# Depthwise convolution accumulated in a PSUM bank block by block, the MLP product kept in PSUM, the conv norm with tokens on partitions, and the mixer's statistics taken early

## The chip, the cores and the metric

The kernel runs on one core of a Trainium2 chip. Five engines each work through their own queue of instructions in order: TensorE (PE, matrix products and transposes), VectorE (DVE), ScalarE (ACT), GpSimd (POOL), and SyncE (SP), which issues the transfers between HBM and the on-chip SBUF. Matrix products land in PSUM, eight banks of 512 float32 columns on 128 partitions. The metric is device time in microseconds of one execution. The kernel before took 2656.0 us, the median of three runs (2652.93 to 2656.13).

## The reference

One layer of a streaming encoder on 2048 prompt frames and on 8 streams of 16 new frames each, 17 tiles of 128 frames in all, width 1024, all in float32. Cut to what matters here:

```python
hn = rmsnorm(x, norm_mix)
q, k, v, a, g = split(hn @ w_in)            # 512, 128, 128, 512, 512 columns
attn = sliding_window_attention(q, k, v)    # 512 wide; chunks of 64 frames, two chunks back, sinks
u = a * sigmoid(g)                          # GLU
c = depthwise_causal(u, conv_w, conv_b)     # 31 taps, 512 channels
c = silu(layernorm(c, ln_g, ln_b))          # over the 512 channels
x = x + concat(rmsnorm(attn, attn_out_g), rmsnorm(c, conv_out_g)) @ w_out
x = x + square(relu(rmsnorm(x, norm_ffn) @ w_up)) @ w_down      # 4096 wide
x = x + (p @ w_ple) * sigmoid(rmsnorm(x, norm_ple) @ w_ple_gate)
y = rmsnorm(x, final_norm)
```

## The kernel before

Every product is made in three passes: each operand is split into a rounded part and its remainder (ACT rounds, POOL or DVE subtracts: `split`, L120 and L121, for weights as for some activations; `transpose_split` for the normalised input), and high by high, high by low and low by high are added up in one PSUM bank. Activations lie with channels on partitions and frames along the free dimension.

The work goes through stages in this order.

- **A** (about 0 to 250 us): six blocks of up to three tiles. Each is normalised, transposed (`tr`), split (`hn`, L258 and L259), written to the scratch tensor `H`, and multiplied by the `a` and `g` columns of `w_in` in four blocks of 128 channels. ACT takes a tanh (`tg`, L303), DVE makes the GLU (`U`, L314). The weights of this and the next stage come through `raw` (SP, L128) and are split as they arrive; those with a gain, by ACT and DVE (L133, L134).
- **B** (250 to 618 us): the q, k, v columns, from `H` read back as `hnb` (L446 issues eight loads to a block), and attention in 32 chunks of 64 frames: scores (`s`), row maximum (L346, DVE), exponentials (L352, ACT), scaling (L381 and L379: on ACT, DVE, and for the chunks from `TAILC` on also on POOL), transposes (`pt`), values (`o`). The result goes to the scratch tensor `M`.
- **C** (590 to 742 us): the output projection by `c_tile` for nine tiles, 48 products to a tile (L538), each with its two statistics of `M` first: ACT squares (`sq`), POOL adds in two steps, PE sums over partitions (`st`, L528), DVE and POOL make the factor (`ors`). After the fourth tile `mlp_front(0)` reads four finished tiles back from `X1`, scales them (L572) and transposes and splits them (`sp`, `hf`) for the first MLP block.
- **MLP** (742 to 2390 us): five blocks (`F_BLOCKS`), each 32 column blocks of `w_up` (`up`) and their part of `w_down` (`d`). ACT makes relu and its square `ht` (L715, L716), DVE multiplies again in full precision (L717: `relu`<-`up`,`relu`) and subtracts for the remainder (L718). L738 adds `d` to the residual. At the end of block 1 `c_late` does the output projection of the other eight tiles (L623), with its own statistics (`sql`, `stl`, `orl`).
- **PLE** (2390 to 2649 us): the gated embedding and the last norm.

The convolution is a generator (`conv_steps`) that other stages advance. A group is four tiles, 512 frames (or the 8 short streams, `US`); a step is one tap for all four channel blocks. Blocks 0 to 2 are on DVE, each with an accumulator `acc` in SBUF (L201 the first tap, L203 the others: `acc` <- `U` times weight plus `acc`). Block 3 (`PCB`) is an ACT product `tap` (L198) and a POOL addition (L199). After 31 taps `conv_post` transposes a tile (`c`, L152), takes mean and variance (L155, L156, `lrs`), normalises on ACT (`z`, L162), transposes back (L165), applies gain and bias (L169 on DVE for the tiles from `TAILZ` on, else L172 on ACT), tanh and a product (L175, L176), and stores to `M`. `A_STEPS` says how many steps follow each channel block in A, `B_STEPS` how many follow an attention chunk; tiles 9 to 12 and 13 to 16 are done in MLP blocks 0 and 1 (`CONV_LATE`). Both `c` tiles of `conv_post` share the one bank of the pool `psc`.

The order on each engine is fixed when the program is built, by a scheduler with its own model of durations and with priorities from the code (`later`, `steps`); the semaphore waits follow from it.

## Time and profile before

| | |
|---|---|
| median of three runs | 2656.0 us (2652.93 to 2656.13) |
| profiled execution, its own time | 2650.91 us |
| its span, first to last instruction | 2649.1 us |
| mean granted TensorE clock | 0.975 of full speed |
| PE busy | 2527.7 us, 95% |
| DVE, ACT, POOL busy | 1391.0, 1081.8, 1178.6 us |

A busy share says how full an engine was over the whole span and not what the end waited for. The chain that ended last does: it follows each instruction back to what released it. The granted clock is TensorE's share of its full speed; where it is below 1, the same products take longer. In a table by windows, the number of PE instructions in a stretch, held against a stretch in which PE never paused, says how much time was lost there.

### The profile page before, as it was taken

The numbers are of one execution on the slowest core, as the hardware profiler recorded it, in microseconds if no ns is written. First come the engines' busy times: TensorE is split into PE (matmuls) and PEld (weight loads), VectorE is DVE, ScalarE is ACT, GpSimd is POOL, SyncE is SP. The second block draws the span as 40 slices with busy tenths as digits, with TensorE's granted clock in tenths as the row PEclk, the third lists the DMA queues.
The fourth block names the chain that finished last, engine by engine and source line by source line (L and its number), as shares of the span: only waits on it lengthen the run. The fifth ranks groups of instructions, "written<-read, shape, count | busy, mean of one in ns | idle before, by whom it ended". The sixth has DMA issues, their size and how long they took to land.

```text
span 2649.1 us, 32895 instructions
## 1 busy us (share of the span) xinstructions
PE 2527.7 (95%) x12609; PEld 2137.6 (81%) x12609; DVE 1391.0 (53%) x1873; ACT 1081.8 (41%) x2037; POOL 1178.6 (44%) x798
## 2 busy tenths in 40 slices
...
GB/s 233 163 87 150 71 95 60 97 52 116 127 183 79 104 89 114 174 103 92 111 80 129 138 176 169 80 112 80 112 173 128 128 127 199 190 192 126 74 84 48
DMA packets 121854, 320.86 MB, mean 121 GB/s; under 512 B 15713, under 2 KB 49249, under 8 KB 121697
## 3 DMA queue, kind: packets, MB, share of 16 engines
...
HBM read 264.43 MB, written 54.29 MB: 120 GB/s over the span
## 4 chain that ended last, share of the span: by engine, by line
PE 82%; DVE 8%; DMA 3%; POOL 2%; ACT 2%; issue 2%; SPq 0%; POOLq 0%; DVEq 0%; ACTq 0%
PE d L732 26%; PE up L268 24%; PE mm L268 10%; PE pg L754 7%; DVE acc L203 5%; PE acc L538 4%; PE accl L623 2%; PE o L398 2%; PE pq L761 2%; PE s L370 1%; POOL acc L199 1%; POOL w L121 1%; DVE ht L718 1%; ACT pr L352 1%; PE pt L392 1%
## 5 line engine op out<-in xcount | busy, mean ns | idle before, releaser
L121 POOL TENSOR_TENSOR w<-raw,w 128x1024 fp32r<-128x1024 f32 x305 | 767.0, 2531 | 656.9 <-ACT w L120 617.4
L732 PE MATMUL d<-w,ht 128*128 128x512 f32 x3264 | 768.6, 393 | 23.6 <-DVE ht L718 20.3
L268 PE MATMUL up<-hf,w 128*128 128x512 f32 (+2 forms) x3840 | 762.5, 357 | 1.1 <-POOL w L121 1.0
L732 PEld LDWEIGHTS d<-w,ht 128*128 128x128 f32 x3264 | 613.0, 189 | 153.7 <-DVE ht L718 23.0
L268 PEld LDWEIGHTS up<-hf,w 128*128 128x128 f32 x3840 | 659.2, 189 | 93.6 <-POOL w L121 1.4
L120 ACT CAST w<-raw 128x1024 fp32r<-128x1024 f32 x330 | 345.6, 1049 | 637.5 <-PE d L732 445.8
L203 DVE SCALAR_TENSOR_TENSOR acc<-U,vec,acc 128x512 f32<-128x512 f32 x360 | 416.9, 1206 | 0.0
L738 DVE TENSOR_TENSOR accf<-d,accf 128x512 f32<-128x512 f32 x272 | 175.2, 685 | 322.7 <-PE d L732 322.2
L718 DVE TENSOR_TENSOR ht<-relu,ht 128x512 fp32r<-128x512 f32 (+2 forms) x160 | 246.1, 1538 | 5.3
L717 DVE SCALAR_TENSOR_TENSOR relu<-up,relu 128x512 f32<-128x512 f32 (+2 forms) x160 | 97.0, 606 | 236.8 <-ACT ht L716 236.5
L199 POOL TENSOR_TENSOR acc<-acc,tap 128x512 f32<-128x512 f32 (+1 forms) x150 | 198.2, 1321 | 38.5 <-ACT tap L198 29.0
L268 PE MATMUL mm<-hn,w 128*128 128x384 f32 (+1 forms) x1152 | 204.5, 335 | 5.8 <-ACT tg L303 3.7
L268 PE MATMUL mm<-hnb,w 128*128 128x256 f32 (+1 forms) x1152 | 180.4, 306 | 21.0 <-DMA hnb<-H 17.6
L268 PEld LDWEIGHTS mm<-hn,w 128*128 128x128 f32 x1152 | 194.3, 193 | 7.0 <-ACT tg L303 4.2
L268 PEld LDWEIGHTS mm<-hnb,w 128*128 128x128 f32 x1152 | 157.7, 195 | 35.3 <-issue 27.2
L715 ACT ACTIVATE relu<-up 128x512 f32<-128x512 f32 (+2 forms) x160 | 84.9, 531 | 196.2 <-PE up L268 193.4
L754 PE MATMUL pg<-w,xg 128*128 128x512 f32 x510 | 125.4, 392 | 0.0
L198 ACT ACTIVATE tap<-U,vec 128x512 f32<-128x512 f32 x120 | 86.1, 725 | 77.5 <-POOL acc L199 77.0
L754 PEld LDWEIGHTS pg<-w,xg 128*128 128x128 f32 x510 | 94.6, 188 | 18.8
L623 PE MATMUL accl<-w,msl 128*128 128x512 f32 x384 | 94.7, 404 | 9.4 <-DVE xcl L628 9.2
L538 PE MATMUL acc<-w,ms 128*128 128x512 f32 x384 | 94.1, 404 | 7.1 <-ACT ms L120 7.1
L623 PEld LDWEIGHTS accl<-w,msl 128*128 128x128 f32 x384 | 73.8, 195 | 25.3 <-DVE xcl L628 9.4
...
## 6 DMA issues: line engine op xcount, KB each, us to landing
raw<-in_w_up SPq DMA_DIRECT2D x160, 512.0 KB, 3.5
raw<-in_w_down SPq DMA_DIRECT2D x160, 512.0 KB, 3.5
...
```

The lines of the kernel that those rows point to most:

```text
L120: nc.scalar.copy(hi, src)
L121: (eng or nc.gpsimd).tensor_tensor(lo, src, hi.bitcast(F32), ALU.subtract)
L199: nc.gpsimd.tensor_tensor(acc, acc, t, ALU.add)
L203: nc.vector.scalar_tensor_tensor(acc, v, w_, acc, ALU.mult, ALU.add)
L268: nc.tensor.matmul(ps, w(wp, k), m[:, ap_, 0:n], start=(i == 0), stop=(i == 3 * KD - 1))
L538: nc.tensor.matmul(ps, ms[:, ap_, k, :], wo[k][:, wp, nh * 512:(nh + 1) * 512], start=(i == 0), stop=(i == 11))
L623: nc.tensor.matmul(pd[nh], ms[h][:, ap_, k, :], wo[4 * h + k][:, wp, nh * 512:(nh + 1) * 512], start=(i == 0), stop=(i == 11))
L717: nc.vector.scalar_tensor_tensor(r[:, 0:n], ps[:, 0:n], 0.0, r[:, 0:n], ALU.max, ALU.mult)
L718: hs = nc.vector.tensor_tensor(ht[:, 1, 0:n], r[:, 0:n], ht[:, 0, 0:n].bitcast(F32), ALU.subtract)
L732: nc.tensor.matmul(pd[nh], hts[f][:, hp, i * P:(i + 1) * P], wds[f][:, wp, nh * 512:(nh + 1) * 512], start=(j == 0), stop=(j == 3 * GRP - 1))
L738: ad = nc.vector.tensor_tensor(xs, pd[nh], xs, ALU.add)
L754: nc.tensor.matmul(pg, xg[ap_][:, k * P:(k + 1) * P], wg[k][:, wp, ns], start=(i == 0), stop=(i == 3 * KD - 1))
```

## The change

- `conv_steps`: the three DVE blocks are no longer advanced together. Their 93 taps are taken in the order block 0, taps 0 to 30, then block 1, then block 2, still three to a step. The running sum is in the bank `c` of `psc` (a new tile for each block), and only the last tap of a block writes `acc` in SBUF. Each tap now reads what the tap just before it wrote. Block 3 stays on ACT and POOL as it was.
- `conv_post`: gain and bias lie as rows (`lnr`, a new 512 KB input that is spread over the partitions and halved on POOL at the start), so the norm, tanh and product are done with tokens on partitions, by three DVE instructions in or out of the bank (L159, L161, L163), with tanh and a square with sum on ACT between. The sum of squares gives the second statistic of the mixer (`ors[:, t, 1]`). Then come one set of transposes back (L169) and one ACT copy.
- `attn_stat`: after each pair of attention chunks, and once for the short streams, ACT squares `mta` into a `pt` bank, DVE sums over four (L450), PE sums over partitions (L452), DVE and POOL make the factor (L453, L454). It is done 17 times.
- `c_tile` and `c_late_front` lose their statistics and read `ors`. `c_tile` takes its inputs from buffers of its own, and `mlp_front(0)` now follows its seventh tile (tile 8 and tile 0 come after it).
- MLP: the product of L717 goes into the `up` bank in place of `relu`, and the subtraction reads it there.
- `A_STEPS` for the last block falls from 2 to 1, and `B_STEPS` becomes two steps after each chunk.

```diff
-A_STEPS = {1: 4, 2: 4, 3: 2, 4: 2, 5: 2}
-B_STEPS = (1, 2)
+A_STEPS = {1: 4, 2: 4, 3: 2, 4: 2, 5: 1}
+B_STEPS = (2, 2)
...
-        nm = cpool.tile([P, 1], F32, name="lnm")
-        nc.vector.scalar_tensor_tensor(nm, mv[:, 0:1], -1.0, rs, ALU.mult, ALU.mult)
+        nc.vector.scalar_tensor_tensor(tp, tp, mv[:, 0:1], lnr[:, 0], ALU.subtract, ALU.mult)
         z = cpool.tile([P, CC], F32, name="z", bufs=1)
-        nc.scalar.activation(z, tp, AF.Identity, bias=nm, scale=rs)
+        nc.vector.scalar_tensor_tensor(z, tp, rs, lnr[:, 1], ALU.mult, ALU.add)
+        nc.scalar.activation(tp, z, AF.Tanh)
+        nc.vector.scalar_tensor_tensor(z, tp, 1.0, z, ALU.add, ALU.mult)
+        ss = cpool.tile([P, 1], F32, name="lss")
+        nc.scalar.activation(tp, z, AF.Square, accum_out=ss)
+        rstd(ors[:, t, 1:2], ss, 1.0 / CC)
         zt = psc.tile([P, CC], F32, name="c")
         for cb in range(4):
             nc.tensor.transpose(zt[:, cb * P:(cb + 1) * P], z[:, cb * P:(cb + 1) * P], ident)
-        zc = cpool.tile([P, 4, P], F32, name="zc", bufs=1)
-        for cb in range(4):
-            if t >= TAILZ:
-                nc.vector.tensor_scalar(zc[:, cb, :], zt[:, cb * P:(cb + 1) * P], g_lg[:, cb:cb + 1],
-                                        g_lb[:, cb:cb + 1], ALU.mult, ALU.add)
-            else:
-                nc.scalar.activation(zc[:, cb, :], zt[:, cb * P:(cb + 1) * P], AF.Identity,
-                                     bias=g_lb[:, cb:cb + 1], scale=g_lg[:, cb:cb + 1])
-        th = cpool.tile([P, 4, P], F32, name="th", tag="z", bufs=1)
-        nc.scalar.activation(th, zc, AF.Tanh)
-        nc.vector.scalar_tensor_tensor(zc, th, 1.0, zc, ALU.add, ALU.mult)
+        zc = cpool.tile([P, 4, P], F32, name="zc", tag="z", bufs=1)
+        nc.scalar.copy(zc.rearrange("p k n -> p (k n)"), zt)
         nc.sync.dma_start(M[t][:, 4:8, :], zc)
...
-        tall = [cpool.tile([P, 512], F32, name="acc", bufs=5) for _ in range(4)]
+        tall = [cpool.tile([P, 512], F32, name="acc", bufs=4) for _ in range(4)]
         accs = [shape(x) for x in tall]
+        def view(cb, j):
+            if tiles[0] == 0:
+                return US[:, cb, :, j:j + DS]
+            return U[c0 // 512][:, cb, c0 % 512 + j:c0 % 512 + j + n]
+
+        own = [(cb, j) for cb in range(4) if cb not in PCB for j in range(KC)]
+        per = len(own) // KC
         for j in range(KC):
-            for cb in range(4):
-                v = US[:, cb, :, j:j + DS] if tiles[0] == 0 else U[c0 // 512][:, cb, c0 % 512 + j:c0 % 512 + j + n]
+            for cb in PCB:
                 w_, acc = cw[:, j, cb:cb + 1], accs[cb]
-                if cb in PCB:
-                    if j == 0:
-                        nc.gpsimd.tensor_scalar(acc, v, w_, g_b[:, cb:cb + 1], ALU.mult, ALU.add)
-                    else:
-                        t = shape(cpool.tile([P, 512], F32, name="tap", align_bytes=ALN))
-                        nc.scalar.activation(t, v, AF.Copy, scale=w_)
-                        nc.gpsimd.tensor_tensor(acc, acc, t, ALU.add)
-                elif j == 0:
-                    nc.vector.tensor_scalar(acc, v, w_, g_b[:, cb:cb + 1], ALU.mult, ALU.add)
+                if j == 0:
+                    nc.gpsimd.tensor_scalar(acc, view(cb, j), w_, g_b[:, cb:cb + 1], ALU.mult, ALU.add)
                 else:
-                    nc.vector.scalar_tensor_tensor(acc, v, w_, acc, ALU.mult, ALU.add)
+                    t = shape(cpool.tile([P, 512], F32, name="tap", align_bytes=ALN))
+                    nc.scalar.activation(t, view(cb, j), AF.Copy, scale=w_)
+                    nc.gpsimd.tensor_tensor(acc, acc, t, ALU.add)
+            for cb, i in own[j * per:(j + 1) * per]:
+                w_ = cw[:, i, cb:cb + 1]
+                if i == 0:
+                    pacc = shape(psc.tile([P, CC], F32, name="c"))
+                    nc.vector.tensor_scalar(pacc, view(cb, i), w_, g_b[:, cb:cb + 1], ALU.mult, ALU.add)
+                else:
+                    nc.vector.scalar_tensor_tensor(accs[cb] if i == KC - 1 else pacc, view(cb, i), w_, pacc,
+                                                   ALU.mult, ALU.add)
             yield
...
+    nc.sync.dma_start(lnr, a["lnr"].partition_broadcast(P))
+    nc.gpsimd.tensor_scalar(lnr, lnr, 0.5, None, ALU.mult)
...
+    def attn_stat(t, mta):
+        sq = psb.tile([P, 512], F32, name="pt").rearrange("p (j n) -> p j n", j=4)
+        nc.scalar.activation(sq, mta, AF.Square)
+        sr = bpool.tile([P, P], F32, name="sra", bufs=1)
+        nc.vector.tensor_reduce(sr, sq.rearrange("p j n -> p n j"), AX.X, ALU.add)
+        st = psb.tile([P, 512], F32, name="pt")
+        nc.tensor.matmul(st[:, 0:1], sr, ones[:, 0:1], start=True, stop=True)
+        nc.vector.tensor_scalar(ors[:, t, 0:1], st[:, 0:1], 1.0 / CC, EPS, ALU.mult, ALU.add)
+        nc.gpsimd.tensor_tensor(ors[:, t, 0:1], ors[:, t, 0:1], mhalf[:, 0:1], ALU.pow)
...
+                attn_stat(1 + (c0 + i) // 2, mta)
     nc.sync.dma_start(M[0][:, 0:4, :], mts)
+    attn_stat(0, mts)
...
-        nc.scalar.activation(sq, mt, AF.Square)
-        s4 = sq.rearrange("p (h k) n -> p h k n", h=2)
-        nc.gpsimd.tensor_tensor(s4[:, :, 0:2], s4[:, :, 0:2], s4[:, :, 2:4], ALU.add)
-        nc.gpsimd.tensor_tensor(s4[:, :, 0], s4[:, :, 0], s4[:, :, 1], ALU.add)
-        st = ps_.tile([P, 512], F32, name="st", **stt)
-        for h in range(2):
-            nc.tensor.matmul(st[:, h:h + 1], s4[:, h, 0], ones[:, 0:1], start=True, stop=True)
-        rs = pl.tile([P, 2], F32, name="ors", bufs=2)
-        nc.vector.tensor_scalar(rs, st[:, 0:2], 1.0 / CC, EPS, ALU.mult, ALU.add)
-        nc.gpsimd.tensor_tensor(rs, rs, mhalf, ALU.pow)
...
-                nc.vector.scalar_tensor_tensor(xs, ps, rs[:, h:h + 1], xs, ALU.mult, ALU.add)
+                nc.vector.scalar_tensor_tensor(xs, ps, ors[:, t, h:h + 1], xs, ALU.mult, ALU.add)
...
-        c_tile(t, opool, ps2, hpool.tile([P, 8, P], F32, name="mt", tag="xnf", bufs=XNB),
-               hpool.tile([P, D], F32, name="xc", tag="xnf", bufs=XNB),
-               opool.tile([P, 2, 8, P], F32R, name="ms", align_bytes=ALN),
-               opool.tile([P, 8, P], F32, name="sq"), dict(bufs=1), dict(bufs=4))
-        if t == F_BLOCKS[0][-1]:
+        c_tile(t, opool, ps2, opool.tile([P, 8, P], F32, name="mt"), opool.tile([P, D], F32, name="xc"),
+               opool.tile([P, 2, 8, P], F32R, name="ms", align_bytes=ALN), dict(bufs=4))
+        if t == F_BLOCKS[1][-2]:
             mlp_front(0, ps2, "sp", 2)
...
-            sq = fpool.tile([P, 4, P], F32, name="sql", tag="relu", bufs=2)
-            nc.scalar.activation(sq, mt[:, 4 * h:4 * h + 4], AF.Square)
-            nc.gpsimd.tensor_tensor(sq[:, 0:2], sq[:, 0:2], sq[:, 2:4], ALU.add)
-            nc.gpsimd.tensor_tensor(sq[:, 0], sq[:, 0], sq[:, 1], ALU.add)
-            nc.tensor.matmul(st[:, h:h + 1], sq[:, 0], ones[:, 0:1], start=True, stop=True)
-        rs = fpool.tile([P, 2], F32, name="orl", bufs=2)
-        nc.vector.tensor_scalar(rs, st[:, 0:2], 1.0 / CC, EPS, ALU.mult, ALU.add)
-        nc.gpsimd.tensor_tensor(rs, rs, mhalf, ALU.pow)
-        return xt, ms, rs
-
-    def c_late_half(h, xt, ms, rs):
+        return xt, ms
...
-                nc.vector.scalar_tensor_tensor(r[:, 0:n], ps[:, 0:n], 0.0, r[:, 0:n], ALU.max, ALU.mult)
-                hs = nc.vector.tensor_tensor(ht[:, 1, 0:n], r[:, 0:n], ht[:, 0, 0:n].bitcast(F32), ALU.subtract)
+                nc.vector.scalar_tensor_tensor(ps[:, 0:n], ps[:, 0:n], 0.0, r[:, 0:n], ALU.max, ALU.mult)
+                hs = nc.vector.tensor_tensor(ht[:, 1, 0:n], ps[:, 0:n], ht[:, 0, 0:n].bitcast(F32), ALU.subtract)
```

What this does to the order is shown at three places. The first is DVE at the end of A, around the last three GLU products (`U_140` before, `U_141` after, buffer `U3` in both). Before:

```order
L314 SCALAR_TENSOR_TENSOR U_140<-tg,mm 128x256
L203 SCALAR_TENSOR_TENSOR acc<-U_137,vec,acc 128x512 x6
L314 SCALAR_TENSOR_TENSOR U_140<-tg,mm 128x256
L203 SCALAR_TENSOR_TENSOR acc<-U_137,vec,acc 128x512 x8
L134 SCALAR_TENSOR_TENSOR w<-raw,vec,w 128x1024
L314 SCALAR_TENSOR_TENSOR U_140<-tg,mm 128x256
```

After, `c` is the bank that holds the running sum:

```order
L320 SCALAR_TENSOR_TENSOR U_141<-tg,mm 128x256
L207 SCALAR_TENSOR_TENSOR c<-U_138,vec,c 128x512 x5
L320 SCALAR_TENSOR_TENSOR U_141<-tg,mm 128x256
L207 SCALAR_TENSOR_TENSOR c<-U_138,vec,c 128x512 x5
L134 SCALAR_TENSOR_TENSOR w<-raw,vec,w 128x1024
L320 SCALAR_TENSOR_TENSOR U_141<-tg,mm 128x256
```

Eighteen taps stood between the first of these GLU products and the last; now there are twelve.

The second place is POOL. Before, the additions of tiles 9 to 12 (`acc`) stand between the weight remainders `w` of MLP block 0:

```order
L195 TENSOR_SCALAR acc<-U_139,vec 128x512
L199 TENSOR_TENSOR acc<-acc,tap 128x512 x2
L121 TENSOR_TENSOR w<-raw,w 128x1024
L199 TENSOR_TENSOR acc<-acc,tap 128x512
L121 TENSOR_TENSOR w<-raw,w 128x1024 x2
L199 TENSOR_TENSOR acc<-acc,tap 128x512
L121 TENSOR_TENSOR w<-raw,w 128x1024
L199 TENSOR_TENSOR acc<-acc,tap 128x512
L121 TENSOR_TENSOR w<-raw,w 128x1024 x2
L199 TENSOR_TENSOR acc<-acc,tap 128x512
```

After, the same additions stand in the last chunks of attention, around the softmax scalings `pr`:

```order
L387 TENSOR_SCALAR pr<-pr,rc 128x192
L200 TENSOR_TENSOR acc<-acc,tap 128x512
L454 TENSOR_TENSOR ors<-ors,mhalf 128x1
L101 TENSOR_SCALAR ors<-lss 128x1
L200 TENSOR_TENSOR acc<-acc,tap 128x512
L102 TENSOR_TENSOR ors<-ors,mhalf 128x1
L387 TENSOR_SCALAR pr<-pr,rc 128x192
L200 TENSOR_TENSOR acc<-acc,tap 128x512 x4
L387 TENSOR_SCALAR pr<-pr,rc 128x192
L200 TENSOR_TENSOR acc<-acc,tap 128x512 x3
L454 TENSOR_TENSOR ors<-ors,mhalf 128x1
L200 TENSOR_TENSOR acc<-acc,tap 128x512 x9
```

and MLP block 0 begins like this:

```order
L121 TENSOR_TENSOR w<-raw,w 128x1024 x3
L101 TENSOR_SCALAR rs_121<-oss 128x1
L121 TENSOR_TENSOR w<-raw,w 128x1024
L102 TENSOR_TENSOR rs_121<-rs_121,mhalf 128x1
L121 TENSOR_TENSOR w<-raw,w 128x1024 x55
```

The thirty additions (and their ACT products) moved from MLP block 0 to the end of B, and five of the six softmax scalings on POOL now have two to twelve of them directly in front. Before, no addition stood between those six.

The third place is PE in C, around the transposes `sp` of `mlp_front(0)`. Before:

```order
L538 MATMUL acc<-w,ms 128x512 x33
L256 MATMUL sp<-ident,xnf 128x128 x32
L538 MATMUL acc<-w,ms 128x512 x34
L528 MATMUL st<-ones,sq 128x1 x2
L538 MATMUL acc<-w,ms 128x512 x14
```

After:

```order
L546 MATMUL acc<-w,ms 128x512 x44
L261 MATMUL sp<-ident,xnf 128x128 x8
L546 MATMUL acc<-w,ms 128x512 x24
L261 MATMUL sp<-ident,xnf 128x128 x4
L546 MATMUL acc<-w,ms 128x512 x4
L261 MATMUL sp<-ident,xnf 128x128 x4
L546 MATMUL acc<-w,ms 128x512 x20
L261 MATMUL sp<-ident,xnf 128x128 x4
L546 MATMUL acc<-w,ms 128x512 x3
L261 MATMUL sp<-ident,xnf 128x128 x4
L546 MATMUL acc<-w,ms 128x512 x45
L273 MATMUL up<-hf,w 128x512 x50
```

The 32 transposes stood in one piece with four tiles of products still to come; now they come in small groups between the products of the last tiles, and the small products `st` are gone.

## Rows read from the trace of the kernel before

**Rows 1.** The page: busy share of PE, and the chain that ended last.

```profile
PE 2527.7 (95%) x12609; PEld 2137.6 (81%) x12609; DVE 1391.0 (53%) x1873; ACT 1081.8 (41%) x2037; POOL 1178.6 (44%) x798
...
PE 82%; DVE 8%; DMA 3%; POOL 2%; ACT 2%; issue 2%; SPq 0%; POOLq 0%; DVEq 0%; ACTq 0%
```

**Rows 2.** By window: bounds, length, busy time of each engine (x instructions), granted clock, DMA.

```profile
140.00:160.00 20.00, 20.00 (x123) 19.93 (x122) 18.50 (x22) 7.78 (x14) 15.21 (x11) 1.00 0.19 70
160.00:180.00 20.00, 13.97 (x61) 13.04 (x60) 19.08 (x18) 11.19 (x21) 15.27 (x10) 0.74 0.12 44
...
229.00:251.00 22.00, 4.07 (x30) 3.69 (x30) 22.00 (x26) 3.81 (x5) 7.69 (x4) 0.68 0.46 149
...
540.00:618.00 78.00, 67.03 (x257) 39.47 (x257) 40.88 (x105) 44.46 (x155) 13.25 (x16) 0.82 0.14 53
618.00:742.00 124.00, 104.55 (x465) 85.14 (x464) 38.43 (x60) 40.79 (x60) 50.64 (x52) 0.89 0.39 132
...
776.00:880.00 104.00, 88.88 (x369) 71.31 (x368) 95.19 (x72) 43.62 (x58) 89.25 (x43) 0.92 0.28 97
880.00:1103.00 223.00, 223.00 (x1010) 184.67 (x1009) 140.12 (x166) 70.33 (x92) 106.12 (x48) 1.00 0.29 101
...
1176.00:1200.00 24.00, 16.80 (x65) 12.82 (x65) 17.15 (x12) 11.92 (x17) 24.00 (x11) 0.86 0.40 144
...
1436.00:1549.00 113.00, 99.05 (x439) 81.48 (x438) 39.54 (x67) 34.24 (x67) 54.69 (x74) 0.94 0.42 145
```

**Rows 3.** DVE by line and form: busy, mean ns of one | idle before, released by.

```profile
L203 DVE SCALAR_TENSOR_TENSOR acc<-U,vec,acc 128x512 f32<-128x512 f32 x360 | 416.9, 1206 | 0.0
...
L738 DVE TENSOR_TENSOR accf<-d,accf 128x512 f32<-128x512 f32 x272 | 175.2, 685 | 322.7 <-PE d L732 322.2
...
L718 DVE TENSOR_TENSOR ht<-relu,ht 128x512 fp32r<-128x512 f32 x96 | 144.8, 1508 | 3.1
...
L542 DVE SCALAR_TENSOR_TENSOR xc<-acc,ors,xc 128x512 f32<-128x512 f32 x32 | 23.4, 748 | 28.6 <-PE acc L538 22.6 <-POOL ors L531 3.3 <-POOL rs L102 2.4
```

**Rows 4.** The taps of L203 alone, in two windows: length, DVE busy (x taps).

```profile
500.00:600.00 100.00, 25.31 (x36) 0.86 0.23 77
...
780.00:870.00 90.00, 61.47 (x34) 0.92 0.27 93
```

**Rows 5.** Timeline at the end of A: start, length, engine, line, what.

```profile
230.13 5.61 POOL L121 TENSOR_TENSOR w<-raw,w 128x1024 fp32r<-128x1024 f32 x2
230.98 7.96 DVE L203 SCALAR_TENSOR_TENSOR acc<-U,vec,acc 128x512 f32<-128x512 f32 x6
...
234.79 0.36 ACT L303 ACTIVATE tg<-mm 128x256 f32<-128x256 f32 x1
...
245.69 0.40 DVE L314 SCALAR_TENSOR_TENSOR U<-tg,mm 128x256 f32<-128x256 f32 x1
...
246.17 4.53 SPq L446 DMA_DIRECT2D hnb<-H  x8
...
250.53 0.98 PE L268 MATMUL mm<-hnb,w 128*128 128x384 f32 x2 [16.29 <-DMA hnb<-H]
```

**Rows 6.** Chain in C, in order of time: start, length, what.

```profile
639.40 11.47 PE acc L538 x50
...
665.90 4.37 DMA xnf<-X
...
684.46 5.67 PE acc L538 x18
```

**Rows 7.** What PE waited for from 1430 to 1552 us: total, times, longest.

```profile
PE accl L623 <- DVE xcl L628: 9.2, 2, 7.0
PE stl L611 <- POOL sql L610: 4.6, 1, 4.6
```

**Rows 8.** Block 3's ACT products and POOL additions by form.

```profile
L199 POOL TENSOR_TENSOR acc<-acc,tap 128x512 f32<-128x512 f32 x120 | 184.2, 1535 | 31.1 <-ACT tap L198 24.0 <-DVE acc L203 0.6 <-ACT va L490 0.3
...
L198 ACT ACTIVATE tap<-U,vec 128x512 f32<-128x512 f32 x120 | 86.1, 725 | 77.5 <-POOL acc L199 77.0
```

26 lines of the change are left out of this document (13 added, 13 removed).

## The prediction

> **What bounds the kernel now.** I read the page's busy shares and its chain first: PE is busy 95% of the span and is 82% of the chain, DVE 8% [rows 1]. So a change that takes no products away can only win back the time in which PE stood or ran at a lowered clock. The table by windows says where that is. A stretch in which PE never paused gives the rate: 1010 instructions in 223 us, 4.53 per us [rows 2]. Held against it (the reader is to see the instruction count, not the busy time, since a lowered clock also stretches busy time):
> - 776 to 880 us (MLP block 0): 369 / 4.53 = 81.5, so 22.5 of 104 us lost; DVE is busy 95.19 of it.
> - 618 to 742 (C): 465 / 4.53 = 102.6, 21.4 lost.
> - 1436 to 1549 (the late output projection): 439 / 4.53 = 96.9, 16.1 lost.
> - 1176 to 1200 (block 1): 65 / 4.53 = 14.3, 9.7 lost.
> - 160 to 180 (A; its shorter products give 123 in the 20 us before): 20 x 61 / 123 = 9.9, 10.1 lost.
> - 229 to 251: PE has little to do; the wait ends at 250.53 with `hnb` [rows 5].
> - 540 to 618 (the end of B): 257 instructions of mixed length at a clock of 0.82; about 11 us idle, more by clock [rows 2].
>
> **The taps.** The by-form view has 360 taps of 512 columns at a mean of 1206 ns, 416.9 us of DVE [rows 3]. That mean hides two prices: 25.31 / 36 = 0.70 us in a window where POOL does little, 61.47 / 34 = 1.81 us in block 0, where POOL is busy 89.25 of 104 us [rows 2, 4]. The subtraction L718, which like a tap takes both its tensors from SBUF, has 1508 ns; L738 and L542, which take one from PSUM, have 685 and 748 ns [rows 3], and L738 runs in that same block. So what is slow is a DVE instruction with two SBUF tensors beside a busy POOL, and after the change a tap has one SBUF tensor and one PSUM tensor.
>
> No row of before shows an instruction of DVE that writes PSUM, nor a tap that reads what the tap just before it wrote. Bounds: 0.685 us (L738) below, 1.81 us (the crowded tap, no relief) above. The nearest row in form is L542 (a pointer scalar, PSUM and SBUF in): 0.748 us; with some hundredths for the wait on the tap before, I take 0.80. 360 x (1.206 - 0.80) = 146 us of DVE go. Nearly all of that lay beside PE's work; it is worth only what PE waited for.
>
> [...]
>
> **The sum, stage by stage, against the profiled execution's 2650.9 us.**
> - 160 to 180: DVE held back GLU and `hn` by runs of taps. At 0.80 in place of the mean of 1.206 a run of six takes 4.8 us for 7.2, and two such runs stand in it; 7 of the 10.1 us come back (bounds 3 and 10).
> - End of A: the eight `hnb` loads stand on SP behind a weight load that waits for DVE, and DVE reaches its last GLU product at 245.69, six taps before it taking 7.96 us from 230.98 on, 1.33 each [rows 5]. Between the first and the last of the three GLU products in the first listing of the change, 18 taps become 12. From 230.98, twelve at 0.80, the GLU products and a weight's remainder (some 2 us) end at about 243 at worst; at best nothing of DVE is late, and POOL's remainders end it at 235.74, just behind the last tanh at 235.15. The 4.53 us of the loads behind that give PE its first product between 240.5 and 247 in place of 250.53: 7 us (3 to 10).
> - B: of the 102 steps of the first three groups (31 taps each and 9 tiles) A does 52 in place of 56, so B gets 50 in place of 46, which hardly counts; what is new is in its last 78 us. Block 3's work for tiles 9 to 12 comes here: 30 ACT products at 0.725 = 22 us beside the 44.46 that ACT has, and 30 POOL additions at 1.535 = 46 us beside 13.25 [rows 2, 8]. Five of the six softmax scalings on POOL stand behind two to twelve additions, and PE's transposes wait for them. In return tiles 5 to 8 are convolved earlier, so DVE is freer. The 17 `attn_stat` add each one ACT square, one DVE sum, a PE instruction of one column; at 0.73 and 0.75 us they fit into what ACT and DVE have idle even at the end of B, 33.5 and 37.1 us of 78 [rows 2], but take `pt` banks. Bounds: +8 us won (the DVE taps are gone) and 25 us lost (twelve additions at 1.535 = 18 us late once, and some products). I take 6 lost.
> - C: the pause from the end of the fourth tile's products to 684.46 comes from storing the tile, reading it back (4.37 us) and the transposes behind it [rows 6]. With two more tiles of products behind `mlp_front(0)` (96 x 11.47 / 50 = 22 us) it is covered, and the adds and `st` products of eight tiles go. Of 21.4 us lost, the wait for the first tile's load at 618 stays: 18 won (10 to 24).
> - Block 0: groups of three taps at 1.81 = 5.4 us stand in front of L717 and L718, which PE waits for; at 0.80 they are 2.4. POOL has no additions left here. 20 of 22.5 us (9 to 22).
> - Block 1: the POOL additions stay, so only the DVE part: 5 of 9.7 (0 to 9.7).
> - Late projection: PE waited 9.2 us for `xcl` and 4.6 for the last `sql` addition [rows 7]. The second goes whole, of the first the part that stood behind the statistics' POOL work. The loads behind the four buffers stay: 10 of 16.1 (4 to 16).
> - L717 and L718: 96 subtractions of 512 columns get a PSUM source, about 0.75 for 1.508 us; PE is full in 880 to 1103 with the old price [rows 2], so nothing beyond the blocks above. What the longer use of an `up` bank costs: L718 now ends earlier than before, so nothing.
> - Conv norm: DVE gets two more instructions of 512 columns for tiles before 9, fewer for the others. Two waits (POOL's root, ACT's tanh) stand in DVE's queue, where before three did for the late tiles. 0.
> - Start: 512 KB more to load while the weights come: 2 lost (0 to 3).
>
> 7 + 7 - 6 + 18 + 20 + 5 + 10 - 2 = 59 us. 2650.9 - 59 = 2591.9; the profiled execution lies 5.1 us below the median of the runs, so on the median's scale 2656 - 59 = 2597 us. All bounds at their good end make 10 + 10 + 8 + 24 + 22 + 9.7 + 16 = 100 us, 2556; all at their bad end 3 + 3 - 25 + 10 + 9 + 0 + 4 - 3 = 1, 2655.
>
> **The rivals.**
> 1. *The tap keeps its price.* One tensor and the weights are still read from SBUF, and if a tap that waits for its forerunner costs 1.2 us, A's and block 0's gains fall to a third, block 1's to nothing. Left: 2 + 3 - 10 + 18 + 7 + 0 + 10 - 2 = 28 us, 2628. For it: no row shows a DVE write to PSUM, and each tap now waits. Against it: L738 and L542.
> 2. *The whole loss comes back.* The end of B gains from the freed DVE instead of losing, and C and the late projection come near their bounds: 2562 to 2570. For it: PE's rows at 880 to 1103 show that nothing else is short. Against it: chains of loads in C and in the late projection that the change leaves.
> 3. *DVE in B becomes the bound: slower.* Taps stand between row maximum, scale and reciprocal of each chunk on an engine that works in order, and 150 of them are a chain now. At 1.5 us for a tap, B's 150 take 150 x 0.80 = 120 us more of DVE than at 0.70; half of it on PE's path is 60 us lost, against 44 won elsewhere (A, block 0 and block 1 at a half, 3 + 3 + 10 + 2, with C's 18, the late projection's 10 and the start's 2 off): 2656 + 16 = 2672. It decides from 44 / 75 + 0.70 = 1.29 us for a tap. For it: the end of B hangs on latency, its clock is 0.82. Against it: DVE is busy only 40.88 of 78 us there [rows 2].
> 4. *The change doesn't do what it says in block 0*, because POOL's weight remainders were the bound there all along: 89.25 of 104 us. Then 10 of the 20 us stay lost: 2607, inside the forecast's range.
>
> **How the numbers follow.** Forecast with rival 4 (2575 to 2615): 0.60. Rival 1 (2615 to 2640): 0.16. Rival 2 (below 2575): 0.13. No change within 0.2% (5 us, about what a measurement can tell): 0.04. Rival 3 and like losses: 0.07. Range 2562 to 2638: it leaves out the best part of rival 2 and all above rival 1. Faster 0.89, same 0.04, slower 0.07.
>
> **What would show it.** Taps of L207 near 0.8 us alike beside a busy and an idle POOL; if they are above 1.2 in block 0, rival 1. PE's counts in MLP block 0 at 4.5 per us throughout. The first `hnb` product between 241 and 247. In C no pause of 20 us, and the stage near 105 us. At the end of B the wait of PE for `pr`: over 10 us more than before means that the term for B is wrong. A stage B (now 367 us) of more than 390 would make the whole forecast wrong.

## The result and the profile after

The changed kernel took 2563.6 us, the median of four runs (2561.82 to 2565.52), against 2656.1 beside it: a ratio of 0.9653, 95% interval 0.9637 to 0.967. The forecast was 2597 us in a range of 2562 to 2638. So the direction was right and the gain larger than forecast, 92.5 us for 59; the time lies at the very edge of the range, below the 2575 to 2615 that the forecast held likeliest.

The page after, its busy shares and its chain:

```profile
PE 2503.8 (98%) x12575; PEld 2120.4 (83%) x12575; DVE 1115.8 (44%) x1874; ACT 1060.9 (41%) x2027; POOL 1084.7 (42%) x783
...
PE 94%; ACT 2%; DMA 2%; DVE 1%; POOL 1%; issue 1%; SPq 0%; POOLq 0%; ACTq 0%; DVEq 0%
```

PE now fills 98% of the span and is 94% of the chain; DVE, 8% of it before [rows 1], is down to 1%. The work by window (length, busy time of each engine (x instructions), granted clock, DMA):

```profile
160.00:180.00 20.00, 20.00 (x126) 19.79 (x125) 16.89 (x27) 16.79 (x29) 17.90 (x18) 1.00 0.46 171
231.00:532.00 301.00, 287.80 (x1786) 230.94 (x1787) 174.41 (x403) 183.70 (x605) 54.91 (x61) 0.97 0.27 87
532.00:620.00 88.00, 69.39 (x268) 41.09 (x267) 40.64 (x99) 64.87 (x183) 52.65 (x60) 0.78 0.17 59
620.00:712.00 92.00, 92.00 (x416) 75.87 (x416) 35.71 (x46) 23.29 (x32) 27.25 (x24) 0.98 0.47 164
780.00:880.00 100.00, 100.00 (x443) 82.81 (x442) 57.04 (x82) 25.17 (x32) 40.05 (x17) 1.00 0.27 90
1374.00:1464.00 90.00, 90.00 (x406) 74.42 (x405) 35.32 (x48) 28.51 (x59) 41.14 (x50) 1.00 0.52 182
```

These answer to [rows 2]: the stretch of A that ran at a clock of 0.74 is full at 1.00, 100 us of MLP block 0 hold 443 instructions, 4.43 per us, C and the late projection have no gap. Only B is worse: at its end, 532 to 620 us, the clock is 0.78 for 0.82, with 64.87 us of ACT and 52.65 us of POOL where there were 44.46 and 13.25, and before that PE is idle for 13 of 301 us.

DVE by line and form:

```profile
L207 DVE SCALAR_TENSOR_TENSOR c<-U,vec,c 128x512 f32<-128x512 f32 x348 | 261.3, 751 | 6.1
L735 DVE TENSOR_TENSOR accf<-d,accf 128x512 f32<-128x512 f32 x272 | 176.1, 686 | 386.7 <-PE d L729 386.1
...
L715 DVE TENSOR_TENSOR ht<-up,ht 128x512 fp32r<-128x512 f32 x96 | 66.3, 691 | 54.2 <-ACT ht L713 51.6
...
L550 DVE SCALAR_TENSOR_TENSOR xc<-acc,ors,xc 128x512 f32<-128x512 f32 x32 | 24.0, 749 | 32.3 <-PE acc L546 31.8
...
L450 DVE TENSOR_REDUCE sra<-pt 128x128 f32<-128x512 f32 x17 | 11.6, 684 | 5.9 <-ACT pt L448 5.9
```

and the taps alone in three windows (DVE busy (x taps)), the second and third in the MLP blocks:

```profile
160.00:240.00 80.00, 43.68 (x58) 0.91 0.47 161
740.00:900.00 160.00, 50.38 (x67) 1.00 0.31 105
1100.00:1400.00 300.00, 62.80 (x84) 1.00 0.31 105
```

The reader is to hold these against [rows 3, 4]: 0.753, 0.752 and 0.748 us for a tap, the same everywhere. The 0.70 and 1.81 us that the prediction reads from [rows 4] are busy time divided by a count. Taps that overlap, or that the edge of the window cuts, make that quotient a little low; by line and form the taps of before in the same two windows have

```profile
L203 DVE SCALAR_TENSOR_TENSOR acc<-U,vec,acc 128x512 f32<-128x512 f32 x36 | 25.4, 746 | 0.0
...
L203 DVE SCALAR_TENSOR_TENSOR acc<-U,vec,acc 128x512 f32<-128x512 f32 x34 | 62.3, 1882 | 0.0
```

So a tap took 746 ns where POOL was busy 10.03 of 100 us and 1882 where it was busy 82.93 of 90, and now takes 751 on average. The subtraction fell from 1508 to 691 ns. What the chain of taps costs is seen from start to start. A run of three in the kernel before and a run of six after, by the timeline:

```profile
544.72 2.05 DVE L203 SCALAR_TENSOR_TENSOR acc<-U,vec,acc 128x512 f32<-128x512 f32 x3
...
204.26 4.71 DVE L207 SCALAR_TENSOR_TENSOR c<-U,vec,c 128x512 f32<-128x512 f32 x6
```

Before, (2.05 - 0.74) / 2 = 0.66 us: each tap started before the last had ended. After, (4.71 - 0.75) / 5 = 0.79 us, so waiting for the tap before costs 0.13 us a link.

The end of A, by the timeline:

```profile
222.50 0.36 ACT L309 ACTIVATE tg<-mm 128x256 f32<-128x256 f32 x1
...
223.83 0.41 DVE L320 SCALAR_TENSOR_TENSOR U<-tg,mm 128x256 f32<-128x256 f32 x1
...
224.32 6.30 SPq L462 DMA_DIRECT2D hnb<-H  x8
...
231.36 0.98 PE L273 MATMUL mm<-hnb,w 128*128 128x384 f32 x2 [9.83 <-DMA hnb<-H]
```

DVE's last GLU product now starts 1.0 us behind the end of its tanh (10.5 us before, [rows 5]); the eight loads follow at once, and 7 us later PE has its first `hnb`, at 231.36 us, earlier than the 241 to 247 that the prediction named as a sign. What PE waits for over the whole run, the two lines that the text uses:

```profile
PE mm L273 <- DMA hnb<-H: 11.9, 4, 9.8
...
PE pt L452 <- DVE sra L450: 8.2, 4, 2.9
```

The gain by stage, from the first and last starts of PE's products (their lines in the trace; us). The two columns of A are up to the last product with `hn`, and from there to the first with `hnb`; B ends with the first product of C on `ms`, C with the first `up`, blocks 0 and 1 with the first product of the late projection.

| run | A | end of A | B | C | blocks 0, 1 | late proj. | rest | span |
|---|---|---|---|---|---|---|---|---|
| before | 234.0 | 16.5 | 373.6 | 118.7 | 693.5 | 112.4 | 1100.4 | 2649.1 |
| after | 221.3 | 10.1 | 388.3 | 92.5 | 662.4 | 88.8 | 1100.3 | 2563.7 |
| e1_taps_sbuf | 230.7 | 12.8 | 406.3 | 92.6 | 662.5 | 88.8 | 1100.2 | 2593.9 |
| e2_before_taps_psum | 222.8 | 9.8 | 360.4 | 120.9 | 663.0 | 115.4 | 1100.2 | 2592.5 |
| e3_product_sbuf | 220.4 | 9.5 | 387.7 | 93.8 | 661.8 | 89.4 | 1100.7 | 2563.3 |
| e4_stats_late | 220.7 | 10.7 | 357.2 | 103.1 | 664.9 | 118.7 | 1100.2 | 2575.5 |
| e5_stat_one_pair_later | 221.5 | 10.5 | 379.1 | 93.4 | 662.2 | 88.8 | 1100.4 | 2555.9 |
| e6_late_adds_held | 220.4 | 10.2 | 383.1 | 93.6 | 662.3 | 88.8 | 1099.2 | 2557.6 |
| e6b_late_adds_held_taps_sbuf | 230.3 | 12.7 | 395.1 | 93.0 | 675.9 | 88.8 | 1100.6 | 2596.4 |
| e6c_held_all_sbuf | 230.8 | 12.7 | 395.9 | 93.5 | 681.4 | 90.6 | 1101.7 | 2606.6 |
| e7_front_after_fourth | 220.7 | 9.5 | 391.5 | 92.3 | 662.2 | 88.8 | 1099.1 | 2564.1 |
| e10_late_stats_in_mlp | 221.7 | 9.3 | 364.0 | 111.7 | 666.8 | 88.8 | 1101.1 | 2563.4 |
| e11_stat_later_adds_held | 221.0 | 10.8 | 370.5 | 93.9 | 662.5 | 88.9 | 1102.8 | 2550.4 |
| e12_front_fourth_shared_xnf | 221.1 | 10.8 | 391.3 | 115.4 | 662.3 | 88.8 | 1099.6 | 2589.3 |

Between the profiled executions 85.4 us went: 12.7 in A, 6.4 at its end, 26.2 in C, 31.1 in the blocks, 23.6 in the late projection, less 14.7 in B. B is the one stage that the change made longer. Among the four kernels of the table whose code for B is the same (after, e3, e7, e12) B varies from 387.7 to 391.5 us, so a few microseconds there say nothing.

The `up` products tell the two blocks apart: from the first of block 0 to the first of block 1, which is the 769th of them, PE took 376.6 us before and 355.8 after, and from there to the late projection 316.9 and 306.6.

### The profile page after: what moved, and what is told of

Same layout as the page of the kernel before. It is cut to its first block, busy times and chain, and to the rows that moved or that the text cites. A ratio compares the mean times of both kernels' runs of the same rounds, so it can differ in the third digit from the quotient of the medians.

```text
span 2563.7 us, 32974 instructions
## 1 busy us (share of the span) xinstructions
PE 2503.8 (98%) x12575; PEld 2120.4 (83%) x12575; DVE 1115.8 (44%) x1874; ACT 1060.9 (41%) x2027; POOL 1084.7 (42%) x783
## 4 chain that ended last, share of the span: by engine, by line
PE 94%; ACT 2%; DMA 2%; DVE 1%; POOL 1%; issue 1%; SPq 0%; POOLq 0%; ACTq 0%; DVEq 0%
PE up L273 29%; PE d L729 29%; PE mm L273 12%; PE pg L751 7%; PE acc L546 4%; PE accl L620 3%; PE o L404 2%; PE pq L758 2%; PE s L376 1%; DMA hnb<-H 1%; PE pt L398 1%; PE tr L661 1%; PE tr L261 1%; PE pt L392 0%; PE up L261 0%
## 5 line engine op out<-in xcount | busy, mean ns | idle before, releaser
L121 POOL TENSOR_TENSOR w<-raw,w 128x1024 fp32r<-128x1024 f32 x305 | 731.5, 2412 | 708.5 <-ACT w L120 707.2
L729 PE MATMUL d<-w,ht 128*128 128x512 f32 x3264 | 759.7, 390 | 0.3 <-ACT ht L713 0.3
L207 DVE SCALAR_TENSOR_TENSOR c<-U,vec,c 128x512 f32<-128x512 f32 x348 | 261.3, 751 | 6.1
L714 DVE SCALAR_TENSOR_TENSOR up<-up,relu 128x512 f32<-128x512 f32 (+2 forms) x160 | 98.9, 618 | 311.9 <-ACT relu L712 311.7
L200 POOL TENSOR_TENSOR acc<-acc,tap 128x512 f32<-128x512 f32 (+1 forms) x150 | 169.3, 1129 | 44.5 <-ACT tap L199 33.9
L715 DVE TENSOR_TENSOR ht<-up,ht 128x512 fp32r<-128x512 f32 (+2 forms) x160 | 97.7, 611 | 109.8 <-ACT ht L713 105.8
L454 POOL TENSOR_TENSOR ors<-ors,mhalf 128x1 f32<-128x1 f32 x17 | 10.5, 616 | 196.3 <-DVE ors L453 196.2
L713 ACT ACTIVATE ht<-relu 128x512 fp32r<-128x512 f32 (+2 forms) x160 | 90.6, 566 | 1.3
```

The lines of the kernel that those rows point to most:

```text
L121: (eng or nc.gpsimd).tensor_tensor(lo, src, hi.bitcast(F32), ALU.subtract)
L200: nc.gpsimd.tensor_tensor(acc, acc, t, ALU.add)
L207: nc.vector.scalar_tensor_tensor(accs[cb] if i == KC - 1 else pacc, view(cb, i), w_, pacc, ALU.mult, ALU.add)
L713: nc.scalar.activation(ht[:, 0, 0:n], r[:, 0:n], AF.Square)
L714: nc.vector.scalar_tensor_tensor(ps[:, 0:n], ps[:, 0:n], 0.0, r[:, 0:n], ALU.max, ALU.mult)
L715: hs = nc.vector.tensor_tensor(ht[:, 1, 0:n], ps[:, 0:n], ht[:, 0, 0:n].bitcast(F32), ALU.subtract)
```

## The experiments

**The sum back in SBUF, alone.** In the changed kernel:

```diff
-                    pacc = shape(psc.tile([P, CC], F32, name="c"))
-                    nc.vector.tensor_scalar(pacc, view(cb, i), w_, g_b[:, cb:cb + 1], ALU.mult, ALU.add)
+                    nc.vector.tensor_scalar(accs[cb], view(cb, i), w_, g_b[:, cb:cb + 1], ALU.mult, ALU.add)
...
-                    nc.vector.scalar_tensor_tensor(accs[cb] if i == KC - 1 else pacc, view(cb, i), w_, pacc,
-                                                   ALU.mult, ALU.add)
+                    nc.vector.scalar_tensor_tensor(accs[cb], view(cb, i), w_, accs[cb], ALU.mult, ALU.add)
```

> The changed kernel with one thing undone: the running sum of a channel block lies in SBUF (acc) again, block by block as after the change. Theory (the price of a tap with two SBUF tensors beside a busy POOL is what held PE in A and in MLP blocks 0 and 1, and the PSUM operand takes it away): taps at 1.2 to 1.8 us where POOL is busy, 0.75 to 0.80 where it is idle, PE short again in A and in block 1 at least; 10 us back in A and 15 to 25 in the blocks, 2590 to 2600 us. Rival (the gain came from the order: block 3's additions moved out of block 0, fewer steps at the end of A): taps slow, but hidden beside PE; 2564 to 2572 us.

It took 2598.0 us, ratio to before 0.9783 (0.9766 to 0.9799). The total is the theory's, its places only in part: of 30.2 us of span, 9.4 + 2.7 are in A, as expected, but the other 18.0 lie in B and none in the blocks. The taps alone, by window (DVE busy (x taps)):

```profile
500.00:600.00 100.00, 20.94 (x29) 0.95 0.27 91
740.00:900.00 160.00, 73.43 (x57) 1.00 0.39 132
1100.00:1400.00 300.00, 123.34 (x90) 1.00 0.32 107
```

Slow again beside POOL, 1.29 and 1.37 us in the blocks (POOL busy 86.53 us of the 155 from 745 on, and 161.92 of 300), and yet PE stayed full there: it was busy for all of both stretches, with 685 and 1331 instructions. In the first window, where POOL is busy 17 of 100 us, the quotient of 0.72 is low for the edges again. By line and form, and in a run of three by the timeline:

```profile
L206 DVE SCALAR_TENSOR_TENSOR acc<-U,vec,acc 128x512 f32<-128x512 f32 x29 | 21.6, 744 | 0.2
...
513.46 2.32 DVE L206 SCALAR_TENSOR_TENSOR acc<-U,vec,acc 128x512 f32<-128x512 f32 x3
```

These taps too wait for the one before, and start (2.32 - 0.75) / 2 = 0.79 us apart: the price of the chain is the same in SBUF and in PSUM.

**The sum in PSUM, alone.** The kernel before with the loop of `conv_steps` as the change's diff has it, nothing else.

> The kernel before with one part of the change: the taps block by block with the running sum in the bank c; norm, statistics, steps, product and C as before. Theory: taps at 0.75 us everywhere, A shorter by 15 to 20 us, block 0 and 1 by 20 to 30, C and the late projection as before; 2610 to 2622 us. Rival (order): within 15 us of before, 2640 to 2656 us.

2594.7 us, 0.9765 (0.975 to 0.978): 62 of the 92 us, more than the theory gave. A and its end are 17.9 us shorter, B 13.2, the blocks 30.5; C and the late projection are 2 to 3 us longer. In this run too the scheduler moved the additions of tiles 9 to 12 from block 0 into B, so these 30.5 us are not the taps' alone.

**The product in SBUF.**

```diff
-                nc.vector.scalar_tensor_tensor(ps[:, 0:n], ps[:, 0:n], 0.0, r[:, 0:n], ALU.max, ALU.mult)
-                hs = nc.vector.tensor_tensor(ht[:, 1, 0:n], ps[:, 0:n], ht[:, 0, 0:n].bitcast(F32), ALU.subtract)
+                nc.vector.scalar_tensor_tensor(r[:, 0:n], ps[:, 0:n], 0.0, r[:, 0:n], ALU.max, ALU.mult)
+                hs = nc.vector.tensor_tensor(ht[:, 1, 0:n], r[:, 0:n], ht[:, 0, 0:n].bitcast(F32), ALU.subtract)
```

> The changed kernel with the product of L714 written to relu in SBUF again. Theory (PE has no short stretch left in the MLP blocks, the taps alone had made them): the subtraction back at about 1.5 us, PE's waits for ht under 3 us, 2563 to 2568 us. Rival (the subtraction's price was half of what PE waited for in the blocks): 2574 to 2588 us.

2567.7 us, 0.9666 (0.9652 to 0.9681), its span 2563.3 for 2563.7: no difference that these runs can tell. The subtraction was back at 1526 ns on average, and blocks 0 and 1 took 661.8 us for 662.4.

**The statistics late again.** `attn_stat` is not called; `c_tile` and `c_late_front` get back the lines that the diff takes from them.

> The changed kernel with the mixer's statistics where they were: no attn_stat in B; c_tile and the late projection take squares, additions and sums themselves. Theory (the statistics were what held PE in the late projection and partly in C, and attn_stat costs PE some 8 us of waits in B): late projection 10 to 18 us longer, C 4 to 10 longer, B 6 to 10 shorter; 2570 to 2582 us. Rival (off the path: buffers and the place of the MLP's front made the gain in C, and the late projection was short for its loads): 2552 to 2562 us, the gain of B alone.

2570.0 us, 0.9679 (0.966 to 0.9697). The total is the theory's, the parts are much larger: the late projection 29.9 us longer, C 10.6, and B 31.1 shorter. B in two windows, up to the last product with `hnb` (512.6 us; after, 531.8) and behind it, and what PE waits for in the late projection:

```profile
231.00:513.00 282.00, 277.58 (x1750) 225.40 (x1751) 166.41 (x372) 174.52 (x584) 47.96 (x49) 0.98 0.29 94
513.00:589.00 76.00, 61.86 (x273) 36.60 (x274) 38.25 (x97) 58.00 (x177) 38.21 (x47) 0.90 0.20 70
```

```profile
PE accl L638 <- DVE xcl L643: 10.8, 2, 8.2
PE stl L626 <- POOL sql L625: 5.1, 1, 5.1
```

282 us for 301 and 76 for 88: of the 31 us that `attn_stat` costs B, 19 lie in the part that has q, k, v products beside the attention, 12 behind it. Length less busy time gives PE's idle time, 18.6 us here and 31.8 after. So 13 of the 31 us are waits of PE and 18 are longer busy time; of these, its own sums take 6.7:

```profile
L452 PE MATMUL pt<-ones,sra 128*128 128x1 f32 x34 | 6.7, 267 | 9.2 <-DVE sra L450 8.2 <-DVE den L363 1.0
```

Beside the other 11 stands the clock, 0.97 and 0.78 after, 0.98 and 0.90 here. The late projection's two waits are those of [rows 7].

**Block 3's additions held in block 0, with the sum in PSUM, in SBUF, and with the product in SBUF as well.** The first edit, on which the other two rest (they add the diffs above):

```diff
-                    nc.gpsimd.tensor_scalar(acc, view(cb, j), w_, g_b[:, cb:cb + 1], ALU.mult, ALU.add)
+                    nc.gpsimd.tensor_scalar(acc, view(cb, j), w_, bias[:, cb:cb + 1], ALU.mult, ALU.add)
...
-        late = conv_steps(CONV_LATE[bi]) if bi in CONV_LATE else iter(())
+        bias = None
+        if bi == 0:
+            bias = cpool.tile([P, 4], F32, name="bias", bufs=1)
+            nc.vector.scalar_tensor_tensor(bias, rs1[:, 0:4], 0.0, g_b, ALU.mult, ALU.add)
+        late = conv_steps(CONV_LATE[bi], bias) if bi in CONV_LATE else iter(())
```

The bias is `rs1` times zero plus `g_b`, so its value is unchanged; but `rs1` is known only behind the last tile of C, and the first addition has to wait for it.

> The changed kernel with the POOL additions of tiles 9 to 12 held back until MLP block 0, by a bias that depends on C's last tile. Theory (with the sum in PSUM DVE no longer minds POOL, so block 0 can carry the additions): blocks 0 and 1 stay at 662 to 668 us, B 5 to 15 us shorter since ACT and POOL are freer at its end; 2550 to 2560 us. Rival (moving the additions out of block 0 is what filled PE there): blocks at 675 to 690 us, 2572 us or more.

> The same as the run before it, with the running sum in SBUF as well: both the additions in block 0 and taps with two SBUF tensors. With the sum in SBUF but the additions in B the blocks were at 662.5 us, so one of two must hold. Theory (it takes both, slow taps and additions beside them, to make PE short): taps at 1.5 to 1.9 us in block 0, blocks 0 and 1 at 678 to 693 us, 2600 to 2620 us. Rival (neither: taking the taps block by block, or the other edits, filled PE): blocks at 662 to 668 us, 2580 to 2592 us.

> The run before it with the MLP product in SBUF too, so that blocks 0 and 1 are as before but for the order of the taps and the norm. Theory (in a block in which DVE is short, the subtraction's 0.8 us more counts too): blocks 4 to 12 us longer than in the run before it, 685 to 695 us. Rival (the product never counts): within 3 us of it.

2560.7 us, 0.9639 (0.9608 to 0.9669); 2597.4 us, 0.9782 (0.9766 to 0.9797); 2609.4 us, 0.9825 (0.981 to 0.984). The first of these times can't be told from the 2563.6 of the changed kernel; its stages can. Block 0 with the additions and the sum in PSUM:

```profile
740.00:840.00 100.00, 100.00 (x443) 82.84 (x442) 59.73 (x87) 44.33 (x59) 75.34 (x44) 1.00 0.30 97
840.00:900.00 60.00, 60.00 (x267) 49.69 (x266) 32.71 (x48) 19.94 (x26) 31.01 (x14) 1.00 0.38 123
```

its taps alone in the first of these windows:

```profile
740.00:840.00 100.00, 35.16 (x47) 1.00 0.30 97
```

and the same with the sum in SBUF:

```profile
740.00:840.00 100.00, 91.12 (x383) 74.37 (x382) 81.09 (x68) 50.21 (x69) 96.93 (x51) 0.95 0.36 119
840.00:900.00 60.00, 60.00 (x267) 49.67 (x266) 43.92 (x47) 19.80 (x26) 31.37 (x13) 1.00 0.35 114
```

```profile
740.00:840.00 100.00, 59.73 (x34) 0.95 0.36 119
```

PE's 443 instructions in 100 us become 383, DVE's 59.73 us become 81.09, and a tap takes 59.73 / 34 = 1.76 us for 35.16 / 47 = 0.75. So in block 0 it takes both, a slow tap and the additions beside it: 662.4 us for the two blocks with neither, 662.5 and 662.3 with one, 675.9 with both. Both together are not enough everywhere. In the first experiment the additions of tiles 13 to 16 ran beside taps of 20.00 / 13 = 1.54 us, and PE had no pause (all of it, then the taps alone):

```profile
1099.00:1142.00 43.00, 43.00 (x191) 35.61 (x190) 30.19 (x29) 21.74 (x30) 42.22 (x24) 1.00 0.42 144
...
1099.00:1142.00 43.00, 20.00 (x13) 1.00 0.42 144
```

What sets this stretch apart from block 0 is not shown. In the third run the product's price counts as well, 5.5 us more, at the low end of the 4 to 12 expected. The edge of the theory for the second run (678 us) was not reached, and its total was below what was expected. The 12.1 us from 681.4 to the 693.5 of before were not taken apart.

**The statistics one pair later.** `attn_stat` of a pair is called behind the next pair's first chunk:

```diff
+    held = []
...
+            if i % 2 == 0 and held:
+                attn_stat(*held.pop())
...
-                attn_stat(1 + (c0 + i) // 2, mta)
+                held.append((1 + (c0 + i) // 2, mta))
...
+    attn_stat(*held.pop())
```

> The changed kernel, with attn_stat of a pair of chunks written behind the next pair's first chunk. Taking the statistics out of B made B 31 us shorter (388.3 to 357.2 us from the first product with hnb to the first product of C). Theory (PE, in order, stands for DVE's sum behind it: its waits for sra are the cost, with the clock they pull down): the sum is long done when PE comes to it, the waits for sra fall from 8 us to under 2, B is 10 to 20 us shorter, 2545 to 2555 us. Rival (the two pt banks and ACT's square, 17 times each, are the cost): B within 6 us, 2558 to 2567 us.

2554.0 us, 0.9618 (0.9599 to 0.9637). B is 9.2 us shorter, between the two. But PE still waited 6.9 us for `sra` (8.2 before the edit), so the theory's reason is not shown: what the later place saves is not that wait. B in two windows, to be held against the second and third row after:

```profile
232.00:524.00 292.00, 279.93 (x1788) 228.16 (x1789) 176.45 (x403) 184.38 (x608) 55.10 (x62) 0.99 0.28 90
524.00:611.00 87.00, 68.02 (x265) 40.28 (x263) 38.36 (x99) 63.75 (x180) 51.01 (x58) 0.79 0.19 67
```

PE's idle time in B is 31.1 us, against 31.8 after. Its busy time went from 357.2 to 348.0 us for the same work, at a granted clock of 0.99 in the first window for 0.97. So the gain is products that ran faster; why the clock was higher is not shown.

**The front at its old place, without and with the old buffers.**

```diff
-        if t == F_BLOCKS[1][-2]:
+        if t == F_BLOCKS[0][-1]:
```

> The changed kernel with mlp_front(0) after C's fourth tile again. With the statistics back in C it was 10.6 us longer (103.1 to 92.5) of the 26 that the change won there. Theory (the rest is the place of mlp_front, whose read back no product covered): the pause of some 20 us comes back, C 12 to 18 us longer, 2575 to 2582 us. Rival (the input buffers of its own did it: without sharing xnf the next tiles are loaded early and cover the pause wherever the front stands): C within 4 us, 2562 to 2568 us.

2563.8 us, 0.9656 (0.9642 to 0.9671): nothing, the rival's case, as long as C has buffers of its own. Then `mt` and `xc` are also taken from `hpool` with the tag `xnf` again:

> The changed kernel with mlp_front(0) after the fourth tile and with C's inputs mt and xc in the four buffers of xnf again, both as before. The place alone cost nothing (C 92.3 for 92.5 us). Theory (the buffers of its own were the rest of C's gain: shared, the next tiles can't be loaded until the front has read its four xnf): a pause of 12 to 20 us between the front's transposes and the next products, C 104 to 112 us, 2575 to 2584 us. Rival (the rest came from the conv norms of tiles 6 to 8, which no longer fall into C): C within 4 us of 92.5, 2562 to 2568 us.

2586.3 us, 0.9742 (0.9725 to 0.9759): C is 23.1 us longer, more than the theory gave. Its chain (start, length, what) shows the pause of before [rows 6] again:

```profile
658.95 0.76 DVE xc L550
...
659.73 2.67 DMA X<-xc
...
662.42 4.24 DMA xnf<-X
...
676.36 3.81 DMA mt<-M
...
681.29 33.86 PE acc L546 x136
```

From the fourth tile's last DVE instruction at 658.95 to 681.29 PE has only the transposes; the next tile's `mt` is loaded when the last of them has freed a buffer. The front behind the seventh tile with shared buffers was not run, so whether the new place alone would have covered the pause is open.

**Two versions drawn from these.** The first holds the additions, shifts `attn_stat` by a pair, and moves the statistics of the eight late tiles into MLP block 0:

```diff
+    def late_stat(t):
+        sq = fpool.tile([P, 4, P], F32, name="sql", tag="relu", bufs=2)
+        nc.sync.dma_start(sq, M[t][:, 0:4, :])
+        nc.scalar.activation(sq, sq, AF.Square)
+        nc.vector.tensor_tensor(sq[:, 0:2], sq[:, 0:2], sq[:, 2:4], ALU.add)
+        nc.vector.tensor_tensor(sq[:, 0], sq[:, 0], sq[:, 1], ALU.add)
+        st = up_ps("stl")
+        nc.tensor.matmul(st[:, 0:1], sq[:, 0], ones[:, 0:1], start=True, stop=True)
...
+            if bi == 0:
+                with later(tc, BEHIND):
+                    late_stat(9 + g)
```

> A version drawn from the runs so far: the changed kernel with the additions of tiles 9 to 12 held until MLP block 0, attn_stat one pair later, and the statistics of the eight late tiles out of B: in MLP block 0, where PE never waits, M is read back and squared by ACT, added by DVE, summed by PE in an up bank. Theory (what attn_stat costs lies in the last part of B, where no q, k, v products cover it): B at 362 to 370 us in place of 388, C 92 to 95, blocks within 4 us of 662, 2536 to 2548 us. Rival (an up bank taken in the middle of the blocks, or the read back, costs what B gains): 2552 to 2562 us.

2557.5 us, 0.9638 (0.9618 to 0.9657), in the rival's range. B gained as expected, 24.3 us, though not for the reason given: only 6.5 of them are over the next version, which keeps the late tiles' statistics in B. A single wait gave most of it back:

```profile
PE stl L614 <- DVE sql L612: 17.2, 1, 17.2
```

The first of these sums stands in PE's queue ahead of the first `up` product, and DVE's addition for it comes late; the chain has a weight's transfer of 7.96 us directly before that addition. Putting the sum later was not tried. The second version has only the held additions and the shift:

> The changed kernel with the two single edits that helped together: attn_stat one pair later (9 us of B) and the additions of tiles 9 to 12 held until block 0 (5 us of B). Theory (they are separate costs of B, one PE's wait for DVE's sum, one ACT's and POOL's load at the end): B at 372 to 376 us, 2548 to 2553 us. Rival (the same idle time, counted twice): B at 378 to 380 us, 2553 to 2558 us.

2546.4 us (2542.15 to 2552.15), 0.9585 (0.9567 to 0.9603): faster than both kernels. B is 370.5 us, 17.8 less than after, where the two edits alone gave 9.2 + 5.2; the 3.4 us between are within what B varies by. Its end:

```profile
530.00:603.00 73.00, 61.58 (x253) 37.44 (x253) 34.57 (x97) 43.24 (x140) 13.95 (x27) 0.83 0.19 69
```

## Why the prediction was right, and where it was wrong

- *What bounds, and the tap.* Right. 0.80 us was taken; 0.751 was measured for one, 0.79 from start to start. The "some hundredths" for the wait were put on top of a tap's length; against taps that needn't wait the chain costs 0.13 us a link, in PSUM as in SBUF. With the sum in PSUM a tap took 751 ns against the 744 with SBUF in a quiet window of the first experiment, 7 ns more, while 0.5 to 1.1 us go in the crowded ones.
- *A.* 7 + 7 forecast, 12.7 + 6.4 measured. The second term was right in place and size. The first was read from one stretch of 20 us, where at most 10.1 could come back; the rest of the 12.7 came from elsewhere in A. Putting the sum back in SBUF took 12.1 of the 19.1 us away, and the sum in PSUM with the taps block by block gave 17.9 without the other edits: the tap's price is shown as the cause of 12.1 at least. What the order of the taps and the fewer steps give was not run by itself.
- *B.* 6 us lost forecast, 14.7 measured, from terms that were each mis-sized. `attn_stat` was costed by idle time of ACT and DVE and put at nothing; it costs 31.1. The freed DVE was put inside a bound of 8; the tap's price alone is worth 18.0 there. The additions moved to B's end, on which the 6 rested, cost 5.2, 8.6 and 11.2 in the three pairs of runs that differ by them (after and e6, e5 and e11, e1 and e6b). They don't cost it by the step forecast: from 532 to 620 us PE waits for no `pr` of POOL. The step that failed is the first: idle time of ACT and DVE was taken to hide the statistics, and it didn't, not even where q, k, v products stand beside them (19 of the 31 us). That each sum is a link more in a chain through every engine, which PE follows, is the likely reason and is argued, not shown: PE's waits for `sra` are 8.2 us. Rival 3 looked at this stage with reason, but what made it longer were the statistics.
- *C.* 18 forecast, 26.2 measured, and not by the step named, that the products behind `mlp_front(0)` would cover the pause. With buffers of C's own the place was worth nothing; the buffers that C no longer shares with the front were worth 23.1, and the statistics 10.6 (the two overlap). The prediction named the buffers of the late projection as a limit and passed over them in C.
- *Blocks 0 and 1.* 20 + 5 forecast, 31.1 measured. Block 0 gave 20.8 of it, near the 20; block 1 gave 10.3, above the 9.7 that the prediction held for all there was. The forecast laid it to the taps' price; the runs show that in block 0 it takes the slow tap and the additions together, so there either the sum in PSUM or the move of the additions would have filled PE. With both back in block 0 (the second and third run with the additions held) the two blocks are still 17.6 and 12.1 us shorter than before; what else held PE there, and in block 1, stays open. Rival 4 (the weights' remainders as the bound there) fell: POOL with the additions back did not hold PE.
- *Late projection.* 10 forecast, 23.6 measured. The term's sentence that the loads behind the four buffers stay was wrong: PE waits for nothing there after. With the statistics back 29.9 us came back.
- *The product, the norm, the start.* The product in PSUM: nothing forecast, nothing measured. The other two were not tried alone; A, with the start in it, shows no loss.

Stage by stage the miss is 26 us, 85.4 for 59; the other 7 lie in where the two profiled executions stand among their runs. Most of it is one habit: 11 to 48% was taken off the time that PE had lost, for waits that were feared behind the known ones. Except in B there were none; rival 2, with its chance of 0.13, is what happened outside B, and the time is in its 2562 to 2570. That it still fell within the stated range is owed to the loss in B, which the prediction sized too small. In C and the late projection the loss itself was also put too low (21.4 and 16.1 us, with 26.2 and 23.6 won), since the count of PE's instructions took the small products of the statistics and of the norm for full ones.
